# One more hole at partitions 48-51 and a moved hole at 44-47 in a row scatter that fills all DMA engines

## The chip, the cores and the metric

The kernel runs on 1 core of one Trainium2 chip. The metric is the device time of one execution in microseconds, the median of several runs; lower is better. Times within a span, taken from the trace, count from the span's start. The span is some 2 us shorter than the device time of the same run (772.8 against 774.87 us for the profiled run of the kernel before). A *mark* is one increment of a semaphore by a DMA; a row or a scatter has *landed* when its last mark has come. A *record* is one packet in the profile.

## The reference

```python
B, N, D = 8, 2048, 2560                     # x: (B, N, D) f32, scores: (B, N) f32
order = np.argsort(scores, axis=1)
ranks = np.argsort(order, axis=1)
out[b_idx, ranks, :] = x                    # row n of batch b goes to row rank[b, n]
```

Each of 16,384 rows of 10,240 bytes is moved to the place that the rank of its score names: 168 MB read and 168 MB written. The ranks cost VectorE some 400 us (400.7 us busy in the trace of the kernel before); the rest is data movement.

## The kernel before: the parts that matter

Rows take one of three ways.

**In bulk through SBUF.** A batch has 8 groups of 256 rows, two on each partition. 58 groups are loaded into one of 8 buffers and scattered from there by two indirect DMAs, one for each of the two rows of a partition. GpSimd issues both, on the trace's queue 0 (the first load alone is SP's).

```python
def scatter(k, j):
    nc.gpsimd.indirect_dma_start(
        out=out_flat, out_offset=bass.IndirectOffsetOnAxis(ap=rank_i[:, col:col + 1], axis=0),
        in_=xb[k % NBUF][:, j * D:(j + 1) * D], in_offset=None, element_offset=b * N * D,
        **(dict(bounds_check=N - 1, oob_is_err=False) if (b, g) in THIN else {}),
    ).then_inc(s_scat[k % NBUF][j], 16)
```

**HBM to HBM ("direct").** The first group of batches 0 to 5 never enters SBUF. SP (queue 1) and ACT (queue 10) copy 128 rows of it each, one DMA a row, in a loop that loads 16 target addresses into registers and issues 16 copies:

```python
with line.eng.Fori(0, half // G) as q:            # half = 128, G = 16
    _, at = nc.values_load_multi_w_load_instructions(rows_i[b][:, bass.ds(half * h + q * G, G)], ...)
    for i in range(G):
        row = b * N + GROUPS[0][0] + half * h + i
        line.eng.dma_start(out=out_bytes[bass.ds(at[i], ROW)],
                           in_=x_bytes[bass.ds(q * (G * ROW) + row * ROW, ROW)]).then_inc(s_rows[line], 16)
```

**Holes ("thin" groups).** In the groups named in `THIN`, four partitions are skipped by both scatters: 2048 is added to their row numbers, so that the bounds check drops them (the trace has 14,784 scattered packets of 10,240 bytes where 116 scatters of 128 rows make 14,848: 64 fewer, 8 for each of the 8 holes). Their 8 rows go HBM to HBM from SP and ACT, which take the groups of the list in turn.

```python
THIN = {**{(b, 4): 48 for b in range(1, B)}, (7, 5): 44}      # (batch, group): first skipped partition
...
line, name = ((sp, ENG.SP), (act, ENG.Activation))[n % 2]     # n: place in THIN
```

A hole takes work from one DMA engine: in the packet chains of the prediction one engine moves 4 packets of 10,240 bytes in each of a hole's two scatters where the others move 8. Each of the 8 rows comes back as 16 packets of 640 bytes and 16 marks, two packets an engine on average. The kernel evens out the 16 engines in this way.

## Time and profile before

| | before |
|---|---|
| device time, 3 runs | 775.36 us (775.35 to 776.25) |
| span of the profiled run | 772.8 us |
| read and written | 168.5 MB and 168.4 MB |
| rows on queue 1 (SP) and queue 10 (ACT) | 800 and 800 |
| last packet of queue 0, 1, 10 | 770.1, 763.6, 761.6 us |

The page's slices tell that the DMA engines are full nearly from beginning to end (9 in 38 of 40 slices), and the queue table what fills them; their lines stand in the prediction below. Each queue's packet count includes a 4-byte packet for each mark (semaphore increment), and one row on queues 1 and 10 is 16 packets of 640 bytes plus 16 marks (12,800 of each for the 800 rows of queue 10).

### The profile page before, as it was taken

To read this page: it belongs to the slowest core of one execution; us is meant where nothing else is said; L and a number is where in the kernel's file an instruction comes from. 1 tells how busy PE (TensorE), PEld (TensorE's weight loads), DVE (VectorE), ACT (ScalarE), POOL (GpSimd) and SP (SyncE) were. 2 spreads that over 40 slices of the span, in tenths; PEclk is the share of its full clock that TensorE was granted. 3 is DMA by queue.
4 is the path that set the end of the run, shared out by engine and by line. 5 is a ranking of instruction groups with operands and counts; after the bars stand their busy time and mean duration, and the time that the engine had idled before them with its cause. 6 is when DMAs were issued, how large, how long until landed. Compare 5 with 4: busy or idle time off the path is not lost.

```text
span 772.8 us, 8228 instructions
## 1 busy us (share of the span) xinstructions
PE 36.2 (5%) x172; PEld 30.4 (4%) x172; DVE 400.7 (52%) x828; ACT 0.0 (0%) x1; POOL 164.6 (21%) x213
## 2 busy tenths in 40 slices
PE   4000020020020020030000000000000000000000
PEld 3000010010010010030000000000000000000000
DVE  5999979979979979979999500000000000000000
ACT  0000000000000000000000000000000000000000
POOL 4114223222213131312112121212121212112100
PEclk8555555555555555565555555555555555555555
DMA  8999999999999999999999999999999999999996
GB/s 358 418 418 420 418 418 418 418 417 418 418 420 417 420 417 417 419 417 419 416 421 421 422 416 426 416 427 417 422 417 424 417 426 415 424 418 424 419 414 283
DMA packets 80898, 320.15 MB, mean 414 GB/s; under 512 B 28968, under 2 KB 54568, under 8 KB 54568
## 3 DMA queue, kind: packets, MB, share of 16 engines
q0 software_dynamic: 29376, 300.82, 91.7%
q1 hardware_dynamic: 25904, 10.93, 5.2%
q10 hardware_dynamic: 25600, 8.24, 4.3%
q14 instruction: 17, 0.14, 0.0%
q8 instruction: 1, 0.02, 0.0%
HBM read 168.49 MB, written 168.43 MB: 436 GB/s over the span
## 4 chain that ended last, share of the span: by engine, by line
DMA 63%; DVE 13%; another core or an unknown queue 9%; POOL 6%; issue 4%; PE 1%; POOLq 0%; SPq 0%
DMA out_dram<-x,rank_i 57%; DVE trash L239 12%; DMA x<-in_x_dram 6%; POOL out_dram L424 4%; POOL x L126 2%; PE ps_all L196 0%; DVE s_all L341 0%; DMA s_in<-in_scores_dram 0%; PE ps_col L175 0%; POOLq L448 0%; DVE rank_i L277 0%; DVE rank L271 0%; DVE rank L265 0%; PE ps_row L300 0%
## 5 line engine op out<-in xcount | busy, mean ns | idle before, releaser
L239 DVE TENSOR_SCALAR_CACHE_REDUCE trash<-s_all,s_col 128x1792 bf16<-128x1792 f32 (+7 forms) x240 | 315.2, 1348 | 4.6
L424 POOL DMA_INDIRECT out_dram<-x,rank_i x116 | 113.4, 977 | 139.6 <-issue 35.0
L126 POOL DMA_DIRECT2D x<-in_x_dram x88 | 49.4, 565 | 436.9 <-DMA out_dram<-x,rank_i 418.5
L239 DVE SCALAR_TENSOR_TENSOR trash<-s_all,s_col,mask 128x256 bf16<-128x256 f32 x128 | 61.6, 482 | 0.0
L196 PE MATMUL ps_all<-ident,s_col 128*128 128x128 f32 x128 | 28.1, 411 | 3.2 <-DVE s_all L341 2.8
L300 PE MATMUL ps_row<-ident,rank 128*1 128x128 f32 x28 | 8.3, 398 | 393.6 <-DVE rank_i L286 386.4
L196 PEld LDWEIGHTS ps_all<-ident,s_col 128*128 128x128 f32 x128 | 26.5, 222 | 4.2 <-DVE s_all L341 3.2
L341 DVE COPY s_all<-ps_all 128x512 f32<-128x512 f32 x32 | 20.2, 685 | 1.5 <-PE ps_all L196 1.1
L239 DVE DVE_READ_ACCUMULATOR trash<-s_all,s_col 128x1 f32 x240 | 19.9, 83 | 0.0
L300 PEld LDWEIGHTS ps_row<-ident,rank 128*1 128x1 f32 x28 | 2.0, 97 | 397.9 <-DVE rank_i L286 389.5
L311 DVE TENSOR_SCALAR thin_i<-ps_row 1x8 int32<-1x8 f32 x8 | 1.2, 154 | 19.0 <-PE ps_row L300 19.0
L239 DVE DVE_READ_ACCUMULATOR trash<-s_all,s_col,mask 128x1 f32 x128 | 10.7, 83 | 0.0
L326 DVE TENSOR_SCALAR rows_i<-ps_row 1x256 int32<-1x256 f32 x6 | 2.5, 412 | 4.1 <-PE ps_row L300 4.1
L183 DVE COPY s_col<-ps_col 128x128 f32<-128x128 f32 x1 | 0.3, 293 | 4.7 <-PE ps_col L175 4.7
L175 PE MATMUL ps_col<-ident,s_in 8*128 8x8 f32 x16 | 2.1, 262 | 3.9 <-DMA s_in<-in_scores_dram 3.9
L286 DVE TENSOR_SCALAR rank_i<-rank,hole 128x2 int32<-128x2 f32 x8 | 2.1, 262 | 0.3
L175 PEld LDWEIGHTS ps_col<-ident,s_in 8*128 8x128 f32 x16 | 2.0, 211 | 3.9 <-DMA s_in<-in_scores_dram 3.9
L277 DVE CAST rank_i<-rank 128x16 int32<-128x16 f32 (+3 forms) x11 | 1.9, 173 | 0.4
L271 DVE TENSOR_TENSOR rank<-rank,acc 128x16 f32<-128x16 f32 (+3 forms) x11 | 1.9, 171 | 0.4
L265 DVE TENSOR_TENSOR rank<-acc,acc 128x16 f32<-128x16 f32 (+3 forms) x11 | 1.9, 170 | 0.4
L156 POOL TENSOR_SCALAR_AFFINE_SELECT mask<-mask 128x256 f32<-128x256 f32 x2 | 0.8, 398 | 0.0
L168 DVE MEMSET acc<- 128x128 f32 x1 | 0.2, 165 | 1.1 <-SPq L102 1.1
(10 smaller groups left out, 1.8 us busy)
## 6 DMA issues: line engine op xcount, KB each, us to landing
x<-in_x_dram POOLq DMA_DIRECT2D x62, 1280.0 KB
x<-in_x_dram POOLq DMA_DIRECT2D x26, 2560.0 KB
out_dram<-in_x_dram ACTq DMA_DIRECT2D x800, 10.0 KB
out_dram<-in_x_dram SPq DMA_DIRECT2D x800, 10.0 KB
x<-in_x_dram SPq DMA_DIRECT2D x2, 1280.0 KB, 9.1
out_dram<-x,rank_i POOLq DMA_INDIRECT x116, 49.0
s_in<-in_scores_dram SPq DMA_DIRECT2D x1, 64.0 KB
```

The lines of the kernel that those rows point to most:

```text
L126: line.eng.dma_start(out=xb[k % NBUF][:, part], in_=rows[:, part]).then_inc(sem, 16)
L175: nc.tensor.transpose(out=ps_col[:, B * c:B * (c + 1)], in_=s_in[:, r + j:r + m * P:m], identity=ident[:B, :B],)
L196: nc.tensor.transpose(out=ps_all[:, P * c:P * (c + 1)], in_=s_col[:, c, b:b + 1].to_broadcast([P, P]), identity=ident[:],)
L239: do(out=trash[i][:, :P * (hi_c - lo_c)], in0=s_all[:, P * lo_c:P * hi_c], accum_out=acc[i][:, col:col + 1], **how,)
L265: nc.vector.tensor_tensor(out=rank[:, cols], in0=acc[0][:, cols], in1=acc[1][:, cols], op=OP.add)
L271: nc.vector.tensor_tensor(out=rank[:, cols], in0=rank[:, cols], in1=acc[2][:, cols], op=OP.add)
L277: nc.vector.tensor_copy(out=rank_i[:, cols], in_=rank[:, cols])
L286: nc.vector.tensor_scalar(out=rank_i[:, cols], in0=rank[:, cols], scalar1=hole[:, i:i + 1], scalar2=None, op0=OP.add,)
L300: nc.tensor.transpose(out=ps_row[:1, P * j:P * (j + 1)], in_=rank[:, col:col + 1], identity=ident[:],)
L326: nc.vector.tensor_scalar(out=rows_i[b][:].rearrange("o (p j) -> o p j", p=P), in0=ps_row[:1, :WIDE].rearrange("o (j p) -> o p j", p=P), s ...
L341: nc.vector.tensor_copy(out=s_all[:, 512 * q:512 * (q + 1)], in_=ps_all[:, 512 * q:512 * (q + 1)],)
L424: nc.gpsimd.indirect_dma_start(out=out_flat, out_offset=bass.IndirectOffsetOnAxis(ap=rank_i[:, col:col + 1], axis=0), in_=xb[k % NBUF][:, ...
```

## The change

The intent: engine A, which serves partitions 48-51, ends last (its last packet at 770.10 us in the prediction's chains). An eighth hole there, at group (2,6), takes 8 more packets from it. The hole at 44-47 goes from group (7,5) to the last group, (7,7). A knob (`FLAT`) to unroll the row loop comes along unused.

```diff
-    THIN = {**{(b, 4): 48 for b in range(1, B)}, (7, 5): 44}
+    FLAT = ()
+    THIN = {**{(b, 4): 48 for b in range(1, B)}, (2, 6): 48, (7, 7): 44}
@@ the row copies
-                with line.eng.Fori(0, half // G) as q:
+                def copies(q):
+                    first = b * N + GROUPS[0][0] + half * h
... (same loads and copies, the source offset written as (first + i) * ROW)
+                if b in FLAT:
+                    for q in range(half // G):
+                        copies(q)
+                else:
+                    with line.eng.Fori(0, half // G) as q:
+                        copies(q)
```

By the list's order SP now has 808 rows and ACT 800.

More of the change, by code (lines that the diff above doesn't have):

```diff
@@ L402 @@
                     for i in range(G):
-                        row = b * N + GROUPS[0][0] + half * h + i
                         line.eng.dma_start(
                             out=out_bytes[bass.ds(at[i], ROW)],
-                            in_=x_bytes[bass.ds(q * (G * ROW) + row * ROW, ROW)],
+                            in_=x_bytes[bass.ds(q * (G * ROW) + (first + i) * ROW, ROW)],
                         ).then_inc(s_rows[line], 16)
+                if b in FLAT:
[4 more added lines that the diff above has]
+                        copies(q)
                 n_rows[line] += half
```

## The prediction

> **What bounds the kernel now.** I read the page's head, its slices and its queue table first, to learn which resource is full.
>
> ```profile
> span 772.8 us, 8228 instructions
> ...
> DVE  5999979979979979979999500000000000000000
> ...
> POOL 4114223222213131312112121212121212112100
> ...
> DMA  8999999999999999999999999999999999999996
> ...
> DMA packets 80898, 320.15 MB, mean 414 GB/s; under 512 B 28968, under 2 KB 54568, under 8 KB 54568
> ## 3 DMA queue, kind: packets, MB, share of 16 engines
> q0 software_dynamic: 29376, 300.82, 91.7%
> q1 hardware_dynamic: 25904, 10.93, 5.2%
> q10 hardware_dynamic: 25600, 8.24, 4.3%
> ```
>
> The DMA row is 9 (90% or more) in 38 of 40 slices, VectorE is done in slice 23 and GpSimd only issues. The three queues add up to 101.2% of 16 engines' span: the records of successive packets overlap by a few ns, so "full" reads slightly over 100%. The long wait in the waits view is therefore the DMA's own backlog, not something to take away:
>
> ```profile
> POOL x L126 <- DMA out_dram<-x,rank_i: 418.5, 45, 11.2
> ```
>
> To see whether the 16 engines are full to the end I asked for the busy share in windows of one microsecond there (the number before GB/s is the mean share of 16 engines):
>
> ```profile
> 755.00:765.00 10.00, 0.00 (x0) 0.00 (x0) 0.00 (x0) 0.00 (x0) 0.00 (x0) 0.50 1.02 418
> 765.00:766.00 1.00, 0.00 (x0) 0.00 (x0) 0.00 (x0) 0.00 (x0) 0.00 (x0) 0.50 0.94 399
> 766.00:767.00 1.00, 0.00 (x0) 0.00 (x0) 0.00 (x0) 0.00 (x0) 0.00 (x0) 0.50 0.27 113
> 767.00:768.00 1.00, 0.00 (x0) 0.00 (x0) 0.00 (x0) 0.00 (x0) 0.00 (x0) 0.50 0.17 72
> 768.00:769.00 1.00, 0.00 (x0) 0.00 (x0) 0.00 (x0) 0.00 (x0) 0.00 (x0) 0.50 0.12 51
> 769.00:770.00 1.00, 0.00 (x0) 0.00 (x0) 0.00 (x0) 0.00 (x0) 0.00 (x0) 0.50 0.05 20
> ```
>
> Full until 765, then 0.27, 0.17, 0.12 and 0.05 of 16 engines: about four, three, two and one. So the time is that of the engine with most work, and the change can win only this ragged edge. If all 16 stopped together they would stop near the mean of these ends.
>
> The records of packets (start, length, queue, size) show who the last ones are, though they carry no engine number: a packet starts about 4 ns before its predecessor's recorded end, so I chained them backwards from the 16 last semaphore writes. Twelve engines end at 765.6 to 766.6 us of the span, one at 767.26, one at 767.71, engine B at 768.98 and engine A at 770.10. Counting data packets between semaphore writes names both: in each of the two scatters of group (7,4), which skip partitions 48-51, A moves 4 packets where the others move 8; in those of (7,5), which skip 44-47, B does. So A serves 48-51 and ends last, and B serves 44-47 and ends 1.11 us earlier. From A's end to the span's end (landing, last waits) is 2.7 us.
>
> [...] one engine falls from 8 to 4 packets, and it is not the same one for the two holes. [...] the last scatter's 16 marks come over 4.6 us, and the slowest decides. [...] short packets of q1 and q10 stand between the 10,240-byte ones of q0. [...]
>
> **The change, part by part.** The holes go from (1,4)...(7,4) at 48 and (7,5) at 44, to the same seven plus (2,6) at 48, and (7,7) at 44.
>
> *Removed.* One queue-0 packet of 10,240 bytes costs its engine 91.7% x 772.8 us = 708.7 us for 300.82 MB / 16 = 18.80 MB, so 386 ns (381 ns from start to start in the chains). The hole of (2,6) takes 4 rows from each of 2 scatters, 8 packets, all from A: 8 x 381 = 3.05 us.
>
> *Added.* 8 rows HBM to HBM[...]. Queue 10 carries exactly such rows, 800 of them: 4.3% x 772.8 = 33.2 us per engine, 41.5 ns a row, and some 33 ns without the overlap of records (two packets of 640 and 4 bytes). 8 x 33 = 0.26 us on every engine. The rows are still loaded, so nothing else falls away.
>
> *Moved.* The hole at 44 stays 8 packets of B and 8 rows. It is in another scatter, and both are issued and queued before B's end; an engine that is never idle ends when its total is done, whatever the order. Worth 0.
>
> *Beside other work.* One more rank addition (262 ns), one more thin_i (154 ns, after a wait of about 3 us for TensorE) and two transposes in batch 2. VectorE has that batch's ranks at 165 us and its thin rows at 170; GpSimd issues the batch's first scatter at 179, after waiting for older scatters, and VectorE is done at 437 us. Hidden. GpSimd issues the same 116 scatters.
>
> *The sum.* A: 770.10 - 3.05 + 0.26 = 767.31. B: 768.98 + 0.26 = 769.24. The next one 767.71 + 0.26 = 767.97. B becomes last, 0.86 us before A's old end. So of the 3.05 us taken from A only 0.86 shows: 775.36 - 0.9 = 774.5, and I choose 774.4, since in the timed runs (775.35 to 776.25, the profiled one 774.87) the excess probably was A's and part of it would go too.
>
> **The rivals.** (1) *The SP queue becomes the tail.* Holes alternate SP, ACT in the order of the list: (2,6) takes the ACT place of (7,5), and (7,7) falls to SP. SP has 808 rows against ACT's 800. It finished issuing 36 us before the end:
>
> ```profile
> 660.14 74.44 ACTq L404 DMA_DIRECT2D out_dram<-in_x_dram  x78
> 660.98 75.99 SPq L404 DMA_DIRECT2D out_dram<-in_x_dram  x80
> ```
>
> At 76.0 / 80 = 0.95 us a row, 8 rows more move its end from 737.0 to 744.6, still before the data's. But SP's last row landed at 764.1; if rows keep coming at 0.95 us, the last lands at 771.7, after A's old end of 770.1, and the time becomes about 777. Against it: once the short packets have no long ones to alternate with, a row needs 33 ns per engine, and all rows are issued 20 us earlier. I expect 767 to 769 for the last row. (2) *The moved hole helps B after all*, because the last scatter is shorter on B just where nothing hides it. Then B ends at 766.2, the rest at 768, and the time is 773.3. Against it: B's total of packets is the same. (3) *Nothing shows:* A's excess varies from run to run by as much as the 0.9 us that separates the three times, or another engine has it; 775.4. (4) *VectorE delays a scatter* in batch 2; the DMA row would have a hole near 190 us. Nothing speaks for it.
>
> **Range and chances.** All mechanisms together reach from 773.3 to 777. The central sum gives 774.4, the spread of runs about 0.5 on either side, rival 2 sets the low end and rival 3 the high one: 773.4 to 775.6 should hold it 8 times in 10. Two per cent is 15.5 us, over three times the whole ragged edge of 4.5 us; within 2% has 0.98, with 0.01 each for faster and slower.
>
> **What would show it.** The span shrinks by about 1 us; q0 has 8 packets fewer (29,368) and q1 256 more. In the microsecond windows the step with one engine alone disappears or shrinks to about the last 1.3 us, and that engine is the one that lacks 4 packets in each scatter of (7,7). A, with the holes at (7,4), ends near 767.3. The slices before stay at 9. I am wrong if A still ends last, if the last packets are 640-byte ones of queue 1, if B's end moves by over 0.6 us although its total has not, or if an idle slice opens anywhere before 765.

## More of the kernel before

In the kernel before, in the first 420 us of the span:

```profile
out_dram<-in_x_dram ACTq DMA_DIRECT2D x452, 10.0 KB
out_dram<-in_x_dram SPq DMA_DIRECT2D x448, 10.0 KB
```

## The result

The changed kernel took 778.29 us (777.44 to 779.5, 4 runs) against 775.37 us: ratio 1.0036, 95% interval 1.0018 to 1.0054. It was expected to gain 1 us and lost 3. A ratio here is the mean time of one kernel's fast runs over that of the other's of the same rounds, so it isn't quite the ratio of the medians.

The page after, head, slices and queue table:

```profile
span 775.6 us, 8254 instructions
...
DMA  8999999999999999999999999999999999999996
...
DMA packets 81154, 320.15 MB, mean 413 GB/s; under 512 B 29104, under 2 KB 54832, under 8 KB 54832
...
q0 software_dynamic: 29376, 300.74, 91.4%
q1 hardware_dynamic: 26160, 11.01, 5.3%
q10 hardware_dynamic: 25600, 8.24, 4.2%
```

Queue 0 moves 0.08 MB less, which is the 8 packets of 10,240 bytes, and queue 1 has 256 packets more, as forecast. Nothing is idle in the middle. The packet count of queue 0 did not fall: the records show that each skipped row leaves a 4-byte packet of 9 ns in its place (72 more of these than marks, 64 before).

The difference is in the tail. The busy share of the 16 engines by the microsecond, of the changed kernel:

```profile
765.00:766.00 1.00, 0.00 (x0) 0.00 (x0) 0.00 (x0) 0.00 (x0) 0.00 (x0) 0.50 0.97 386
766.00:767.00 1.00, 0.00 (x0) 0.00 (x0) 0.00 (x0) 0.00 (x0) 0.00 (x0) 0.50 1.07 270
767.00:768.00 1.00, 0.00 (x0) 0.00 (x0) 0.00 (x0) 0.00 (x0) 0.00 (x0) 0.50 0.74 140
...
769.00:770.00 1.00, 0.00 (x0) 0.00 (x0) 0.00 (x0) 0.00 (x0) 0.00 (x0) 0.50 0.05 15
770.00:771.00 1.00, 0.00 (x0) 0.00 (x0) 0.00 (x0) 0.00 (x0) 0.00 (x0) 0.50 0.08 8
771.00:772.00 1.00, 0.00 (x0) 0.00 (x0) 0.00 (x0) 0.00 (x0) 0.00 (x0) 0.50 0.01 1
```

From 766 to 768 the engines are busy (1.07 and 0.74, against 0.27 and 0.17 before) at only 270 and 140 GB/s: busy with small packets. Whose, the queue table from 766 us to the end tells, first of the kernel before:

```profile
q0 software_dynamic: 36, 0.26, 8.9%
```

and of the changed kernel:

```profile
q1 hardware_dynamic: 464, 0.15, 12.9%
q0 software_dynamic: 50, 0.28, 7.2%
q10 hardware_dynamic: 185, 0.06, 2.4%
```

Before, both row queues were empty by 766. Now SP's holds 464 packets and ACT's 185, though ACT has no row more than before. SP's waits agree: in the changed kernel it waits for its rows at the end (third line from its view of waits):

```profile
SPq L416 <- DVE rows_i L329: 15.2, 1, 15.2
SPq L28 <- DMA out_dram<-x,rank_i: 14.0, 5, 3.6
SPq L105 <- DMA out_dram<-in_x_dram: 3.8, 1, 3.8
```

In the kernel before that wait is not in the list, and SP ends with the wait for the scatters:

```profile
SPq L28 <- DMA out_dram<-x,rank_i: 33.1, 8, 12.5
```

And the rows were late long before the end. The changed kernel's row issues in the first 420 us:

```profile
out_dram<-in_x_dram SPq DMA_DIRECT2D x436, 10.0 KB
out_dram<-in_x_dram ACTq DMA_DIRECT2D x436, 10.0 KB
```

12 and 16 fewer than before, at a time when nothing of the change but the hole of (2,6) in its scatters and rank arithmetic had been reached (the eighth hole's own rows are issued only with batch 5's). After 420 us the distance stays: between 420 and 720 us, ACT's queue moved 308.7 rows before and 308.8 after, counting records. So both kernels run there at one fixed rate, and what is late at 420 us is still late when queue 0 runs dry.

### The profile page after: what moved, and what is told of

The parts are those of the page before. It is cut to its first block, busy times and chain, and to the rows that moved or that the text cites. A ratio compares the mean times of both kernels' runs of the same rounds, so it can differ in the third digit from the quotient of the medians.

```text
span 775.6 us, 8254 instructions
## 1 busy us (share of the span) xinstructions
PE 35.5 (5%) x174; PEld 30.1 (4%) x174; DVE 401.2 (52%) x830; ACT 0.0 (0%) x1; POOL 165.2 (21%) x213
## 4 chain that ended last, share of the span: by engine, by line
DMA 63%; DVE 13%; another core or an unknown queue 10%; POOL 6%; issue 3%; PE 1%; POOLq 0%; SPq 0%
DMA out_dram<-x,rank_i 57%; DVE trash L242 12%; DMA x<-in_x_dram 6%; POOL out_dram L434 4%; POOL x L129 2%; DVE s_all L344 0%; PE ps_all L199 0%; DMA s_in<-in_scores_dram 0%; PE ps_col L178 0%; POOLq L458 0%; DVE rank_i L280 0%; DVE rank L274 0%; DVE rank L268 0%; PE ps_row L303 0%
```

## The experiments

There were 15 runs of 13 kernels, in four sets, each set on a chip of its own beside runs of the kernel before; the first runs of the changed kernel, above, belong to none of them. Theory T, to begin with: the time is lost to rows outliving queue 0. R1: the moved hole does it, in queue 0. Later T2, which says in addition that the lateness differs from run to run. R2, R3 and R4 are rivals that the expectations state where they come up.

### First set: fewer rows, one half of the change at a time

`e1_after_less32`: the changed kernel without the last 16 rows of each row queue in batch 5. 32 output rows stay unwritten, so it is wrong.

```diff
-                    with line.eng.Fori(0, half // G) as q:
+                    with line.eng.Fori(0, half // G - (b == 5)) as q:
...
-                n_rows[line] += half
+                n_rows[line] += half - G * (b == 5)
```

> The changed kernel without the last 16 rows that SP and the last 16 that ACT copy HBM to HBM for batch 5 (32 output rows stay unwritten: wrong on purpose). Theory T (the tail of short packets): in the changed kernel queue 1 and queue 10 still hold rows when queue 0 is empty; their packets end at 771.4 us of the span and their marks land until 774.3, where queue 0 ends at 769.8. With 16 rows fewer on each queue both are done before queue 0 and the time falls by over 3 us, to 773.0 to 774.8. Rival R1 (the moved hole is to blame through queue 0) or R2 (the whole kernel is slower by chance of code placement): only the work of 32 rows goes, 32 x 33 ns = 1.1 us, so about 777.2.

Measured: 773.26 us (773.08 to 773.69), 0.9973 of before. From 766 us on, only queue 0 is left:

```profile
q0 software_dynamic: 32, 0.17, 6.1%
```

The number is as T says, but the test turned out weak. In its trace 438 and 438 rows had started by 420 us, so it was not late like the changed kernel's first trace, and no unedited changed kernel ran beside it; in the next set that one took 773.73 us. The time is 1.1 us below the predicted 774.4, about the work of the missing rows.

`e2_before_less32`: the same edit to the kernel before, also wrong.

> Control: the same 32 rows left out of the kernel before (wrong on purpose). All theories: there the short packets end 6.5 us before queue 0 does, so only their work goes, 32 x 33 ns = 1.1 us: 774.3, at most 775.4 if rows weigh less than worked out.

Measured: 774.07 us (773.22 to 774.67), 0.998. 32 rows fewer are worth 1.4 us where there is no tail. The changed kernel's 773.26 is 5.0 us under its first 778.29, but that is a difference between sets, and after `e7_after_again` it can't be put down to the 32 rows alone.

`e3_add_only`:

```diff
-    THIN = {..., (2, 6): 48, (7, 7): 44}
+    THIN = {..., (2, 6): 48, (7, 5): 44}
```

> Only the hole at 48-51 of group (2,6) is added; the hole at 44-47 stays at (7,5). Theory T: SP has 808 rows as in the changed kernel, so the tail of short packets is there: 777 to 779. R1 (the moved hole): no move, so the forecast of the prediction holds, about 774.5.

Measured: 775.15 us, single runs 774.77, 776.3, 778.24, 774.88, 775.03, 775.26; ratio 1.0006 (0.9993 to 1.0018). A miss for T as it stood: 808 rows alone don't make the tail each time. In its trace (774.77 us) 452 and 443 rows had started by 420 us, 15 to 24 more than in the changed kernel's first trace, although the two programs are the same up to batch 7's ranks. That made T into T2.

`e4_move_only`:

```diff
-    THIN = {..., (2, 6): 48, (7, 7): 44}
+    THIN = {..., (7, 7): 44}
```

> Only the hole at 44-47 is moved from (7,5) to (7,7); 800 rows on each queue as before. Theory T: no more rows than before, so 775.0 to 776.0. R1: as the changed kernel, 777.5 to 779.

Measured: 775.3 us (775.18 to 775.37), 0.9997. The move alone costs nothing; R1 falls.

### Second set: the same kernel again, a lead, a delay

`e7_after_again`: the changed kernel, no edit.

> The changed kernel unaltered, beside the others on one chip: is its 778 there each time, or does it depend on the run as add-only's times (774.8 to 778.2) suggest? Theory T2: the time depends on how far the SP and ACT rows are behind at 420 us of the span, which is decided by what the two issuers lose before; with 808 rows and little luck 777 to 779.5, in lucky runs 775. R1 (the moved hole): 777.5 to 779.5 in every run.

Measured: 773.73 us (773.53 to 775.33), 0.9983. The very same program is now faster than before, and faster than T2 allowed (775 in lucky runs). R1 falls once more. The rows still set the end of its profiled run: the last landed at 770.7 us, 1.5 us after the last scatter.

`e5_flat_all`: row loops of all six batches unrolled.

```diff
-    FLAT = ()
+    FLAT = range(6)
```

> The changed kernel with its row copies unrolled (no loop, so fewer address instructions between two copies); same rows, same holes. Theory T2: the rows are issued faster before 420 us, are never behind, the short packets end before queue 0, and the time is what the prediction worked out from queue 0 alone: 773.8 to 775.0. R1: the moved hole is still there, 777.5 to 779.5.

Measured: 777.05 us (776.68 to 777.17), 1.002. A miss for T2 (773.8 to 775.0), and just below what R1 said. The rows did get their lead: the last landed at 731.8 us. But queue 0 now ended late, at 772.7 us. The queue table shows the price, 35 instruction fetches where there were 17:

```profile
q14 instruction: 35, 0.29, 0.1%
```

A late fetch of 8 KB takes 0.309 us by its record. In the last groups' scatters one engine lands 6.1 us after the median and gains at neither hole, so it is neither A nor B; 18 more fetches of 0.31 us are 5.6 us (the later expectation says 19). That these fall to one engine was not shown: records carry no engine number, and in the kernel before, with 17 fetches, one engine is 3.8 to 6.0 us after the median in its last groups too.

`e8_before_delay`: the kernel before, batch 1's rows held back until VectorE's 34th instruction after their numbers are ready, about 11 us (in the trace SP's issues pause for 10.2 us at 139.5 us).

```diff
-                line.after(dve, t_rows[b])
+                line.after(dve, t_rows[b] + (34 if b == 1 else 0))
```

> The kernel before, with the row copies of batch 1 held back on SP and ACT until VectorE is in the middle of batch 2, about 11 us or 13 rows; nothing else differs. Theory T2: the rows never catch up, the short packets of queues 1 and 10 outlive queue 0, and the kernel before becomes slow like the changed one: 777 to 780. Rival (the rows do not matter, the holes do): 775.3 as before.

Measured: 777.75 us (777.29 to 778.1), 1.0031 (1.0018 to 1.0045), all five runs above the highest of the kernel before beside it (775.59). The issues in the first 420 us and the queues from 766 us on look like those of the changed kernel:

```profile
out_dram<-in_x_dram ACTq DMA_DIRECT2D x438, 10.0 KB
out_dram<-in_x_dram SPq DMA_DIRECT2D x424, 10.0 KB
```

```profile
q1 hardware_dynamic: 326, 0.10, 20.3%
q0 software_dynamic: 25, 0.19, 7.0%
q10 hardware_dynamic: 69, 0.02, 1.3%
```

This experiment carries the argument: no hole was touched, rows were made late at 140 us, they landed last, and the end came 2.4 us later. So late rows alone are enough for the tail.

`e9_add_only_delay`: the same delay in `e3_add_only`.

> Only the hole at (2,6) added (that ran at 775.15), with the same hold of about 11 us on batch 1's rows. Theory T2: 777 to 780 in all runs. R1 (it takes the hole moved to (7,7)): about 775.

Measured: 776.01 us, runs 780.39, 775.31, 777.06, 775.6, 775.03, 776.43. Only partly as forecast: two of six lay in 777 to 780.4. The one profiled (780.39) had started 412 and 413 rows by 420 us, and its last row landed at 777.3, 9.3 us after the last scatter. The lateness isn't set by the delay alone. And this is a point against T2 as it stands: with 8 rows more and the same delay, five of six runs were faster than all five of `e8_before_delay`. They have no trace, so why stays open.

### Third set: can the rows get a lead cheaply?

`g_after_g32` (changed kernel), `g_before_g32` (kernel before), `g_add_g32` (only the hole of (2,6) added), each with

```diff
-    G = 16
+    G = 32
```

> The changed kernel with loops of 32 rows instead of 16 (half as many loads of row numbers on SP and ACT, each 1.0 to 2.8 us; few more instructions, so few more instruction fetches). Theory T2: the rows are done before queue 0, and the time is the queue-0 sum of the prediction in every run: 773.7 to 775.0, spread under 1 us. Rival R3 (unrolled was slow because early rows take something from queue 0, not because of its 19 more instruction fetches): 776.5 to 777.5.

> The kernel before with loops of 32 rows. Theory T2: its rows were not what ended last, so 775.0 to 775.8 as without; the gap to the changed kernel with the same loops is then the change without its rows' tail, 0.5 to 1.5 us. Rival (more time for rows is good by itself): falls as much as the changed kernel does.

> Only the hole at (2,6) added, loops of 32 rows. If moving the hole at 44-47 is worth 0, as the prediction has it: equal to the changed kernel with loops of 32 within 0.5 us. R1 (the move does something in queue 0): more than 1 us away from it.

Measured: 774.44 us (774.27 to 774.75), 0.9978; 775.88 us (775.42 to 776.09), 0.9994; 774.67 us (774.46 to 776.98), 0.9987. The numbers are as T2 forecast (the kernel before by 0.08 us above its range), but the means was not what I took it for. One load of 32 row numbers takes twice as long as one of 16, here in the kernel before and then with the larger loop:

```profile
L393 SPq TENSOR_LOAD <-rows_i x48: 976/1194/2612, 18.1 to 721.6; - x48
```

```profile
L397 SPq TENSOR_LOAD <-rows_i x24: 1867/2332/4923, 18.3 to 714.4; - x24
```

(minimum, median and maximum in ns). The shortest load of 8 numbers in the trace of before took 0.53 us, of 16 there 0.98 and of 32 here 1.87 us, some 56 ns for each further number. So no issue time is saved on loads. By 420 us of its trace ACT had 455 rows started and SP 437; SP's last packet came at 769.85 us, just beside queue 0's 769.86. Among these three, the changed kernel is 1.4 us below the kernel before, and the moved hole is worth 0.2 us by medians, which is nothing against the runs' spread.

`g_after_flat0`: the changed kernel, only batch 0's row loop unrolled.

```diff
-    FLAT = ()
+    FLAT = (0,)
```

> The changed kernel with the row copies of batch 0 alone unrolled. Theory T2: rows some 10 ahead at 120 us of the span and so ahead at the end; some 3 to 4 more instruction fetches [...]: 773.7 to 775.2. R3: 776 and more.

Measured: 773.37 us (773.1 to 773.65), 0.9962 (0.9948 to 0.9975). 123 and 122 rows had started at 120 us, against 105 and 106 in the changed kernel's first trace. The time is 0.3 us below its forecast. The lead did not last in this trace: by 420 us it had 439 and 439 rows started, no more than the kernel before, and its last row landed 0.2 us before its last scatter.

In this set the kernel before itself had one run at 779.83 us among ten, the others 775.69 to 776.97, so it may fall into the tail too; there is no trace of that run.

### Fourth set: what was still open

`h_after_third`: the changed kernel, no edit, a third loading.

> The changed kernel unaltered, a third time. The first time all 4 runs were at 777.4 to 779.5, the second time 5 runs at 773.5 to 775.3. Theory T2 (rows late by luck of the issuers): a mixture, between 773 and 780, and the profiled run's span is the larger of last scatter's landing + 2.2 us and last row's landing + 1.3 us. Rival R4 (the first time was one bad loading of the program): all near 774.

Measured: 775.04 us (774.49 to 775.47), 0.9994. Neither the first time's 778.3 nor the second's 773.7. In the profiled run the last row landed at 772.3, 1.1 us after the last scatter, and T2's rule for the span held. Its mixture "between 773 and 780" did not come: the five runs lie within 1.0 us, which is nearer to R4 (the first loading was a bad one). For T2 speak `e3_add_only` and `e9_add_only_delay`, whose runs of one loading spread over 3.5 and 5.4 us. Whether the loading or the single run decides the lateness stays open.

`h_before_flat0`: the holes of the kernel before, batch 0 unrolled (the edit of `g_after_flat0` with the old `THIN`).

> The kernel before's holes with the row copies of batch 0 unrolled: control for the best version. Theory T2: engine A still has one hole less, so 774.6 to 775.8, 1 to 2 us above the changed kernel with the same unrolling (773.4). Rival (the unrolling alone is the gain): 773 to 774.

Measured: 774.23 us (773.44 to 774.74), 0.9984. Lower than forecast by 0.4 us, and 0.2 us above what the rival said (773 to 774, the unrolling alone is the gain): the unrolling alone gave about 1 us to the kernel before. Its trace has the rows done at 751 us and the last scatter at 770.3, only 0.3 us earlier than in the trace of before, so where the rest of that 1 us comes from stays open.

`h_after_flat0_2`: `g_after_flat0` again, beside the two.

> The changed kernel with batch 0's row copies unrolled, again beside these two. Theory T2: 773.0 to 774.5 with a spread under 1 us, as the first time (773.1 to 773.65).

Measured: 773.74 us (773.16 to 774.02), 0.9977 (0.9963 to 0.999). With a lead for the rows the change is worth 0.5 us by medians in this set (773.74 against 774.23); the runs overlap (773.16 to 774.02 and 773.44 to 774.74).

### What the traces say together

From each trace, in us of the span: rows started by 420 us on queue 1 / queue 10 (640-byte packets divided by 16), the landing of the last row and of the last scatter, and the span.

| run | rows by 420 | last row | last scatter | span |
|---|---|---|---|---|
| before (800 / 800 rows) | 438 / 442 | 764.1 | 770.6 | 772.8 |
| after (808 / 800) | 428 / 428 | 774.3 | 770.5 | 775.6 |
| e7_after_again | 429 / 437 | 770.7 | 769.2 | 772.0 |
| h_after_third | 435 / 442 | 772.3 | 771.2 | 773.6 |
| e3_add_only | 452 / 443 | 762.7 | 770.7 | 772.9 |
| e4_move_only (800 / 800) | 437 / 438 | 765.3 | 771.0 | 773.3 |
| e8_before_delay (800 / 800) | 417 / 428 | 774.4 | 771.1 | 775.6 |
| e9_add_only_delay | 412 / 413 | 777.3 | 768.0 | 778.5 |
| e5_flat_all | 489 / 488 | 731.8 | 773.0 | 775.2 |
| g_after_g32 | 437 / 455 | 770.2 | 770.4 | 772.6 |
| g_after_flat0 | 439 / 439 | 769.4 | 769.6 | 771.8 |

In every row the span is, within 0.2 us, the larger of "last row + 1.3" and "last scatter + 2.2"; the six runs left out obey it too. So there are two streams that both must end. The change adds rows to one of them and takes packets from the other.

The rows that SP still has to start at 420 us (all its rows less those started) nearly order the last landing in the traces where SP's row lands last: 362 to 364 left in the kernel before, `e4_move_only` and `g_before_g32`, landing at 764.1 to 766.0 us; 369 to 371 left in `g_after_g32`, `g_add_g32` and `g_after_flat0`, at 769.4 to 770.2; 373 to 396 in the changed kernel's three traces and the two with a delay, at 770.7 to 777.3. Eight rows more and a late start thus act alike.

**Why lateness is not made good before queue 0 runs dry.** From 420 us on the loads are of 20,480 bytes. A group of 256 rows is then, on one engine on average, 8 load packets, 16 scatter packets and 3 marks: 27 turns of queue 0 in 13.1 us. The records of the kernel before show that queues 1 and 10 get one short packet each for such a turn: of 1,757 large packets of queue 0 between 500 and 560 us, 99% have a packet of queue 1 starting 3 or 4 ns before their end, over 99% of queue 1's packets there have one of queue 10 at that place, and over 99% of queue 10's have one of queue 0; the three queues have 1,990, 1,990 and 1,989 packets in these 60 us. A row needs two such turns of an engine (32 packets, data and marks, over 16 engines): 13.5 rows in 13.1 us, or 309 in 300 us. That is the 308.7 and 308.8 measured.

**What makes it vary.** Until some 398 us the loads are of 10,240 bytes and a group has more turns (36 in about 13.3 us; at one short packet a turn, as counted above, that is room for some 40 rows in 30 us, an estimate), and from 120 us on the rows started at only 29 to 37 in 30 us, less where e8 and e9 held them back: there the issuers set the pace. In seven traces (before, after, e3, e4, e7, e8, e9) a load of 16 row numbers on SP or ACT that began before 420 us took 2.15 us on average when it overlapped a DMA issue of GpSimd or began within 2.7 us of its end (144 loads), and 1.12 us otherwise (240 loads). One pass of SP's loop of 16 rows takes 13.9 to 15.7 us on average there and GpSimd's cycle of one group 13.2 to 13.3 us, so a loop that has come into step with GpSimd's burst may stay in step for long. The first half of this is measured; that it decides a run is an inference from it, and no run took GpSimd's issues away.

## Why the prediction was wrong, point by point

- **"the time is that of the engine with most work".** Incomplete. It is that of the last stream. With two streams only the larger shows, and in the kernel before the row queues were done just 2 us before the first engines ran out of queue 0 (763.6 against 765.6 us). By the rule above its rows had 7.4 us in hand (764.1 + 1.3 against 772.8).
- **Removed and moved.** Right in kind. Queue 0 fell by 8 packets, the move alone was worth nothing (e4, and g_add_g32 against g_after_g32), and where the rows didn't set the end the sum came out: 774.44 us with loops of 32 against 774.4 predicted, 773.26 us without 32 rows against 774.4 - 1.06. That the sums agree is in part luck, for it isn't always B that ends last. Chained back from the last packet, the last engine moves 4 packets in each scatter of (7,7) in `e1_after_less32`, so it is B (768.68 us). In `h_after_flat0_2`, where the rows were done at 758 us, it moves 8, so it is not B (769.20 us). The forecast of 29,368 packets was wrong, because a skipped row leaves a 4-byte packet.
- **A's and B's ends.** B was forecast at 769.24 us, and the last packet of queue 0 came at 769.82 in the changed kernel; among the rows' packets its trace doesn't tell plainly which engine that was. The engines' excess isn't constant: what packets of 10,240 bytes last beyond 385 ns adds up, over all 16 engines, to 27 to 36 us in the seven traces named above.
- **Added: 33 ns a row and engine.** About right as work while long packets run (32 rows were worth 1.4 us in `e2_before_less32`, 1.06 forecast). Wrong as the cost in the tail, where marks land one by one: the last five marks of SP's queue in the changed kernel land at 773.55, 773.74, 773.93, 774.12 and 774.31 us, 0.19 us apart and up to 2.9 us after the last packet (771.40).
- **The step that failed** is the dismissal of rival 1: "Against it: once the short packets have no long ones to alternate with, a row needs 33 ns per engine, and all rows are issued 20 us earlier. I expect 767 to 769 for the last row." The last row landed at 774.3, and the time was 778.3, where the rival as I wrote it said 771.7 and "about 777". The sign named for it came: the last packets, up to 771.4 us, were those of queue 1. I took the rows' position from one trace as if it were fixed, and let only SP's 8 rows move it; both queues were 10 to 14 rows behind at 420 us in that run, and why is not shown. But that is not all. In `h_after_third` the rows were hardly late (435 and 442, against 438 and 442), and SP's last row still landed at 772.3, 8.2 us later than in the kernel before. In `g_after_g32`, `g_add_g32` and `g_after_flat0`, with 437 to 439 on SP, it landed at 769.4 to 770.2. So the 8 rows themselves moved the last landing by 5 to 8 us, where the dismissal allowed 3 to 5 (from 764.1 to 767 to 769). The rival's own 777 was no sound sum either: it set the landing of a row against the last packet of A and let A's 2.7 us follow. By the rule above a row that lands at 771.7 gives a span of 773.0 and some 775 us, as `h_after_third` did (772.3 and 775.47). The first loading's 778 took the lateness as well.

  In its trace the issues ended at 755.9 us on SP and 749.6 on ACT, where I had worked out 744.6 and seen 734.6:

```profile
699.56 56.38 SPq L407 DMA_DIRECT2D out_dram<-in_x_dram  x62
700.11 49.45 ACTq L407 DMA_DIRECT2D out_dram<-in_x_dram  x49
```

- **Range.** Rival 1 reached 777 in the text, yet the range ended at 775.6. Three loadings of the same changed kernel gave medians of 778.29, 773.73 and 775.04 us: two within the range, the first outside. The spread of the kernel before (0.9 us), which I used for both, belongs to a kernel whose rows just get done in time; over the edge the spread is 6 us.
- **Within 2%.** Right, and not in doubt.

The best version found is the changed kernel with batch 0's row copies unrolled: 773.37 and 773.74 us on two loadings, 0.9962 and 0.9977 of before. The unedited changed kernel had 773.73 on its best loading; what the unrolling adds is that all ten runs lay between 773.1 and 774.02.

## What to carry to other kernels

When an engine is never idle, list every stream that must end, with its own margin, before working out a gain on one of them. In every trace here the span was, within 0.2 us, the larger of "last row + 1.3 us" and "last scatter + 2.2 us", so the balance by small side copies could shorten it only while the rows' sum stayed the smaller one. The row queues got one packet per turn beside queue 0 (99% of its large packets), which held each to 309 rows in 300 us before and after the change: what was late at 420 us stayed late, so a lead had to come before that. And where a result hangs on such a margin, load the kernel more than once before calling a difference of a few tenths of a per cent its own.
